# Three plain items instead of two in each up stage, and a scaling row moved to the delta net's output projection

## The chip, the cores and the metric

The kernel runs on one core of a Trainium2 chip. Its engines each work through their own list of instructions in order and meet at semaphores: TensorE (PE, matrix products), VectorE (DVE), ScalarE (ACT), GpSimd (POOL) and SyncE (SP, which here only issues transfers). The metric is the device time of one execution in microseconds.

## The reference

A trunk of two layers over a sequence of 1024 positions with 1024 features, all in float32. Each layer is a mixer and a feed-forward block, both with a residual and a layer norm whose scale, shift and output gain come from a conditioning vector ("ada"):

```python
FFN_HIDDEN = ((8 * D_MODEL // 3 + 255) // 256) * 256   # 2816
FFN_CONV = 3
```

Layer 0 mixes with a gated delta net (projection, causal convolution, chunked recurrence, output projection), layer 1 with a retention. The feed-forward block makes two products of the normalized activations with the up weights, a gate half and an up half of 2816 features each. The gate goes through a causal convolution over three positions and a silu, is multiplied with the up half, and the result goes through the down weights. What the change touches is the up product, and the conditioning's output gain row of layer 0's feed-forward block, a product of the conditioning vector with a 1024 x 1024 part of the ada weights.

## The kernel before

**Arithmetic.** A float32 operand is held as two parts, high and low. `split` (L87 to L90) makes them: ACT copies the high part (L89), DVE subtracts it from the source (L90). `mm3` (L109 to L112) multiplies two such operands with three matmuls of 128 x 128 by 128 x 512.

**Stages** (us in the profiled execution): prologue to 87; delta net to 640; its output projection (`proj_ln`, matmuls at L324) 642 to 771; the first layer's up stage 771 to 1200; its down product (`proj_gen`, L1454) to 1440; retention to 2290; the second layer's up stage 2290 to 2725; its down product to 2952.

**The up stage** is `strassen` (L1173). The activations are cut into blocks of 4 tiles each, called "11", "21", "12", "22" (features by halves of the sequence). The weights come in 22 items, each with two units `ua`, `ub` of 512 KB; `pair_items` lists for each of 11 pairs a gate item and then an up item. An item's four output tiles are made in one of two ways.

- A *plain* item is `side(n, 0)` and `side(n, 1)`. A side multiplies both units (loaded and split whole by `load_w`) with "11" and "21", or with "12" and "22": 2 units x 8 tiles x 3 = 48 matmuls, 96 for both sides.
- `wino` makes an item of 7 block products of 12 matmuls, 84 together, by the scheme of Strassen and Winograd. It needs sums of weight blocks (`psub`, recorded at L1229), a split of each of the seven blocks (`wb`, L89 and L90 again), copies of partial results (L1240) and adds. Four of its products take T1 to T4, sums of activation blocks.

The order at the stage's start: first side of items 1 and 0 (each copied aside by ACT), then `build_T` (L424 to L475), which makes "12" and "22" and returns `rest()`, which makes T1 to T4 tile by tile; second side of item 0; `rest()`; second side of item 1; `wino` for items 2 to 21. T1 and T2 are allocated under the same tag ("hTb", 8 buffers) as "12", so their tiles for k = 2 and 3 are written into buffers of "12" once its last product is over. After a gate item stands its convolution (`conv`, L1573 to L1585: ACT at L1578 and L1584, two L1583 on DVE for each of four tiles), with an up item the product with the gate (L1597) and sums for the down product (L1604). In `wino` the matmuls of a product stand at L110 to L112, or at L1179 where they are added onto an open sum; a gate item's adds are at L1569.

**Work in the background.** `bg_ada` (L219 to L262) queues small units that make the conditioning's rows and columns. A row has two halves of 512 features. For each half eight tiles of 512 KB are loaded by SP (L225) into a tile `mvw` whose tag is `bg_tag[0]`, and DVE adds them up with the vector's entries as scalars (one L235, seven L237); a product with ones sums over the partitions (L259, in plain float32, recorded as two matmuls) and a copy puts the row aside (L260). The queue is worked off one unit at each `bg_step` (L113), two to each `wino` item. `bg_ada(0, 5, "row")` is queued after the output projection and so is done within the first eight of those units; in the first layer four columns of layer 1 (`bg_ada(1, j, "col")`) come behind it.

A scheduler fixes the order of each engine's instructions when the program is built, from the order in which they are written and its estimate of when they are ready; the source order alone doesn't tell it.

Of the kernel before, what the change touches and what calls it, by code (L numbers as in the profile page):

```python
# [24 lines left out]
NF = F // P  # L25
# [8 lines left out]
def trunk_kernel(ctx: ExitStack, tc, A):  # L34
# [82 lines left out]
    bg_tag = ["wr"]  # L117
# [76 lines left out]
    def vcol(name):  # L194
        a, n = VC[name]
        return vc[:, a:a + n]
# [22 lines left out]
    def bg_ada(i, j, kind):  # L219
        box = {}  # L220

        def unit(nh, kp):
            wr = tl(bg_tag[0], [P, 2, HALF], name="mvw")
            c0 = j * D + nh * HALF
            sp.dma_start(wr, A["ada_w"][i, kp * 256:(kp + 1) * 256, c0:c0 + HALF].rearrange("(a p) n -> p a n", p=P))  # L225
            return 2 if bg_tag[0] == "xT" else 1, lambda: work(nh, kp, wr)

        def work(nh, kp, wr):
            if kp == 0:
                box["a"] = tl("ada", [P, HALF])  # L230
            a = box["a"]
            for kk in range(2):
                k = kp * 2 + kk
                if k == 0:
                    dve.tensor_scalar(a, wr[:, 0], e[:, 0:1], None, ALU.mult)  # L235
                else:
                    dve.scalar_tensor_tensor(a, wr[:, kk], e[:, k:k + 1], a, ALU.mult, ALU.add)  # L237
            if kp < KT // 2 - 1:
                return
            if kind == "col":  # L240
                if nh == 0:
                    vecs[i, j] = ct(f"v{i}{j}", [P, KT])
                gs = slice(4 * nh, 4 * nh + 4)
                v, b = vecs[i, j][:, gs], bias_cols(i, j)[:, gs]
                tp, pt = bg_ps[0](), tl("sm2", [P, 4], name="cs")
                for g in range(4):
                    pe.transpose(tp[:, g * P:(g + 1) * P], a[:, g * P:(g + 1) * P], ident)
                for g in range(4):
                    act.activation(a[:, g * P:(g + 1) * P], tp[:, g * P:(g + 1) * P], AF.Copy, accum_out=pt[:, g:g + 1])
                if j in (1, 2, 4):  # L250
                    dve.scalar_tensor_tensor(v, pt, 1.0, b, ALU.add, ALU.add)
                else:
                    dve.tensor_add(v, pt, b)
            else:
                if nh == 0:
                    rows[i, j] = row_load(A["ada_b"][i:i + 1, j * D:(j + 1) * D], ("x", i))
                g = rows[i, j][nh]
                pt = bg_ps[0]()
                pe.matmul(pt, ones, a, start=True, stop=True)  # L259
                dve.scalar_tensor_tensor(g, pt, 1.0, g, ALU.add, ALU.add)  # L260

        for nh in range(2):  # L262
            for kp in range(KT // 2):
                bg.append(lambda nh=nh, kp=kp: unit(nh, kp))
# [290 lines left out]
    xT = {}  # L555
# [614 lines left out]
        dve.tensor_tensor(b, a, b, ALU.add)  # L1170
        return b

    def strassen(hT0, xts, scale, shift, items, tags=("hTb", "hTb", "qkv", "qkv", "aux"), direct=False):  # L1173
        B = {"11": hT0[:4], "21": hT0[4:]}
        nblk = [0]
        nacc = [0]

        def mm_on(*a, **kw):
            return pe.matmul(*a, skip_group_check=True, **kw)  # L1179

        held = {}

        def side(n, s):
            out = []
            for u in items[n][:2]:
                w = held.pop(u.offset, None) or load_w(u)
                if n == 0 and s == 0:
                    held[u.offset] = w
                X = acc_tile()
                for i, b in enumerate((("11", "21"), ("12", "22"))[s]):  # L1190
                    for k in range(4):
                        mm3(X, w, k + 4 * i, B[b][k], i == 0 and k == 0, i == 1 and k == 3)
                out.append(X)
            return out

        ahead, sinks = {}, {}
        for n in (1, 0):
            X = side(n, 0)
            if direct:
                sinks[n] = items[n][2]()  # L1200
                for i in range(2):
                    sinks[n](2 * i, X[i], None)
                continue
            ahead[n] = [tl("cv", [P, 516], name="ah")[:, 0:HALF] for _ in range(2)]
            for t, x in zip(ahead[n], X):
                act.activation(t, x, AF.Copy)
        rest = build_T(B, xts, scale, shift, tags)

        def block(src):
            n = nblk[0]  # L1210
            nblk[0] += 1
            t = tl(("wh", "wl")[n % 2], [P, 2, HALF], F32R, name="wb")
            split(t[:, 0], t[:, 1], src)
            return kn(t[:, 0]), kn(t[:, 1])

        def prod(src, b, onto=None):
            w = block(src)
            if onto is None:
                nacc[0] += 1
                acc = (acc_tile, acc_tile, sc_tile)[nacc[0] % 3]()  # L1220
            else:
                acc = onto
            for k in range(4):
                mm3(acc, w, k, B[b][k], onto is None and k == 0, k == 3, mm_on if onto is not None else pe.matmul)
            return acc

        def psub(x, y, op=ALU.subtract):
            t = mm_tile()
            dve.tensor_tensor(t, x, y, op)  # L1229
            return t  # L1230

        def wino(n, sink):
            ua, ub = items[n][:2]
            wa, wb = tl("wr", [P, D]), tl("wr", [P, D])
            sp.dma_start(wa, ua)
            anchor["wi"] = sp.dma_start(wb, ub)
            a11, a12, a21, a22 = wa[:, hs(0)], wa[:, hs(1)], wb[:, hs(0)], wb[:, hs(1)]
            def copy_of(X, tag="cv"):
                t = tl(tag, [P, 516] if tag == "cv" else [P, HALF], name="pc")[:, 0:HALF]
                act.activation(t, X, AF.Copy)  # L1240
                return t

            X = prod(a11, "11")
            p1 = copy_of(X)
            s1 = psub(a21, a22, ALU.add)
            sink(0, prod(a12, "21"), p1)
            s2 = psub(s1, a11)
            Z = prod(s1, "T1")
            z5 = copy_of(Z)
            s4 = psub(a12, s2)  # L1250
            prod(s2, "T2", X)
            u2 = copy_of(X)
            s3 = psub(a11, a21)
            prod(s4, "22", Z)
            sink(1, Z, u2)
            bg_step()
            prod(s3, "T3", X)
            u3 = copy_of(X, "t2")
            sink(3, X, z5)
            sink(2, prod(a22, "T4"), u3)  # L1260
            bg_step()
            if n > 4:
                row_step()

        bg_tag[0] = "lane"
        for n in range(2):
            if not direct:
                sinks[n] = items[n][2]()
                for i in range(2):
                    sinks[n](2 * i, ahead[n][i], None)  # L1270
            X = side(n, 1)
            for i in range(2):
                sinks[n](2 * i + 1, X[i], None)
            if n == 0:
                rest()
            if items[n][3]:
                items[n][3]()
        for n in range(2, len(items)):
            wino(n, items[n][2]())
            if items[n][3]:  # L1280
                items[n][3]()
        bg_tag[0] = "wr"
        return B
# [249 lines left out]
    def layer_tail(i, mix, wout, xsrc, x_mid, x_out, ln_next, final):  # L1533
        sc2, sh2 = fold(i, 1, 2 * i)
        if i == 0:
            hT0 = []
            get = out_hl(mix)
            G1 = rows[0, 2]
            xts = proj_ln(0, GH, get, wout, xsrc, G1, ("x", i))
            hooks = ln_hooks(0, xts, "hTa", lambda: (sc2, sh2), hT0, x_mid, ("mid", i), BAL["gh"])  # L1540
            xts = proj_ln(1, GH, get, wout, xsrc, G1, ("x", i), hooks=hooks)
            hooks = ln_hooks(1, xts, "hTa", lambda: (sc2, sh2), [], x_mid, ("mid", i))
            for h in hooks[KT:]:
                h()
        else:
            mix.append((sc2, sh2))
            hT0, xts = proj_st(mix[0])
        bg_ada(i, 5, "row")
        bg_gain(2 * i, x_mid, xg[i + 1], "xT")
        if i == 0:  # L1550
            for j in (1, 0, 4, 3):
                bg_ada(1, j, "col")
        cw = vcol(f"ffn_conv{i}")
        cb = vcol(f"ffn_convb{i}")
        ad = dr.tile([NF // 2, 7, P, HALF], F32, tag=f"ad{i}", name=f"ad{i}")
# [51 lines left out]

            return [(up[4 * fp], up[4 * fp + 2], gate_start, conv), (up[4 * fp + 1], up[4 * fp + 3], up_start, None)]

        strassen(hT0, xts, sc2, sh2, [it for fp in range(NF // 2) for it in pair_items(fp)])  # L1610
        while rowq or rowp:
            row_step()
        slots = {"c": "hTa", "x": "qkv"}
# [23 lines left out]
    h0, xts = layer_tail(0, raws, A["gdn_wout"], xin, xs[0], xs[1], next0, False)  # L1637
# [337 lines left out]
```

## Time and profile before

| | |
|---|---|
| runs, us | 2944.8, 2956.14, 2954.41 (median 2954.41) |
| the profiled execution's own time, us | 2954.0 |
| its span in the trace, us | 2952.2 |
| mean granted TensorE clock | 0.982 |
| loads of the ada weights | 80 of 512 KB, 40.96 MB of 344.11 MB read |

The page gives busy times of one execution by engine and the chain of work that ended last, which is followed back from the last instruction to what released it. A timeline row has the start, the duration, the engine, the source line (often that of a helper), the operation with its output and inputs, its count, and in brackets the time that the engine stood idle before it with who ended that. A row of the windows has, for a stretch of time, the busy time of each engine, the granted clock (PEclk, 1.00 is full), and the transfers' share and rate.

### The profile page before, as it was taken

The numbers are of one execution on the slowest core, as the hardware profiler recorded it, in microseconds if no ns is written. First come the engines' busy times: TensorE is split into PE (matmuls) and PEld (weight loads), VectorE is DVE, ScalarE is ACT, GpSimd is POOL, SyncE is SP. The second block draws the span as 40 slices with busy tenths as digits, with TensorE's granted clock in tenths as the row PEclk, the third lists the DMA queues.
The fourth block names the chain that finished last, engine by engine and source line by source line (L and its number), as shares of the span: only waits on it lengthen the run. The fifth ranks groups of instructions, "written<-read, shape, count | busy, mean of one in ns | idle before, by whom it ended". The sixth has DMA issues, their size and how long they took to land.

```text
span 2952.2 us, 38981 instructions
## 1 busy us (share of the span) xinstructions
PE 2822.2 (96%) x13638; PEld 2306.3 (78%) x13638; DVE 2212.5 (75%) x3973; ACT 1316.4 (45%) x2413; POOL 494.4 (17%) x517
## 2 busy tenths in 40 slices
PE   8999898999999999998999999999999899999997
PEld 7787777887787888887878877777777788888886
DVE  5788787656688888958686665666779787777779
ACT  4745565444544444545333332221344544445543
POOL 0312221100013332000000012422202023331001
PEclk9999999999999999999999999999999999999999
DMA  7232222253255655855343364655673353334853
GB/s 277 86 108 68 83 79 80 83 166 138 93 178 173 213 187 191 300 156 176 130 140 121 115 217 154 210 170 164 186 242 125 106 168 128 136 129 161 293 182 114
DMA packets 248276, 459.40 MB, mean 156 GB/s; under 512 B 23632, under 2 KB 77136, under 8 KB 248080
## 3 DMA queue, kind: packets, MB, share of 16 engines
q1 hardware_dynamic: 215680, 405.27, 41.8%
q10 hardware_dynamic: 29760, 43.00, 4.0%
q0 software_dynamic: 2640, 8.65, 0.8%
q8 instruction: 107, 1.75, 0.3%
q14 instruction: 89, 0.73, 0.1%
HBM read 344.11 MB, written 112.72 MB: 155 GB/s over the span
## 4 chain that ended last, share of the span: by engine, by line
PE 73%; DVE 13%; DMA 6%; ACT 4%; issue 2%; POOL 1%; SPq 0%; POOLq 0%; ACTq 0%; DVEq 0%
PE acc L667 15%; PE acc L1179 9%; PE acc L110 5%; PE acc L111 5%; PE acc L112 5%; PE sc L1179 4%; PE sc L667 4%; PE acc L1454 3%; PE mm L667 3%; PE sc L111 2%; PE sc L112 2%; PE sc L110 2%; DVE o L1583 1%; PE mm L1454 1%; PE sc L1454 1%
## 5 line engine op out<-in xcount | busy, mean ns | idle before, releaser
L667 PE MATMUL acc<-hT,wh 128*128 128x512 f32 x960 | 300.2, 394 | 0.0
L1454 PE MATMUL acc<-bb,ab 128*128 128x512 f32 x984 | 236.7, 399 | 12.1 <-DVE bb L90 10.5
L1454 PEld LDWEIGHTS acc<-bb,ab 128*128 128x128 f32 x984 | 186.4, 191 | 56.1 <-DVE bb L90 15.5
L1179 PE MATMUL acc<-T,wb 128*128 128x512 f32 x840 | 203.2, 391 | 6.3 <-DVE wb L90 6.2
L667 PEld LDWEIGHTS acc<-hT,wh 128*128 128x128 f32 x960 | 182.3, 190 | 34.1
L89 ACT ACTIVATE ab<-ar 128x512 fp32r<-128x512 f32 x210 | 130.1, 626 | 166.5 <-PE mm L301 47.8
L667 PE MATMUL acc<-hT,wl 128*128 128x512 f32 x480 | 201.3, 419 | 0.0
L90 DVE TENSOR_TENSOR ab<-ar,ab 128x512 fp32r<-128x512 f32 x210 | 148.5, 713 | 65.2 <-ACT ab L89 65.2
L409 POOL TENSOR_TENSOR xg<-xg,gb 128x512 f32<-128x512 f32 x48 | 62.6, 1304 | 776.3 <-DMA xg<-xs 453.1
L1179 PEld LDWEIGHTS acc<-T,wb 128*128 128x128 f32 x840 | 156.7, 188 | 43.6 <-DVE wb L90 9.0
L90 DVE TENSOR_TENSOR wl<-wr,wh 128x1024 fp32r<-128x1024 f32 x95 | 119.8, 1262 | 88.3 <-ACT wh L89 88.1
L90 DVE TENSOR_TENSOR wb<-wr,wb 128x512 fp32r<-128x512 f32 x162 | 115.8, 720 | 71.5 <-ACT wb L89 71.4
L89 ACT ACTIVATE wh<-wr 128x1024 fp32r<-128x1024 f32 x95 | 100.7, 1061 | 146.4 <-PE acc L667 66.9
L90 DVE TENSOR_TENSOR wb<-mm,wb 128x512 fp32r<-128x512 f32 x216 | 145.8, 684 | 26.5 <-ACT wb L89 25.7
L1604 POOL TENSOR_TENSOR o<-o 128x512 f32<-128x512 f32 x80 | 111.7, 1405 | 287.6 <-ACT pc L1240 190.0
L1583 DVE SCALAR_TENSOR_TENSOR o<-g,vc,o 128x512 f32<-128x512 f32 (+2 forms) x176 | 154.7, 896 | 5.3 <-ACT o L1578 4.7
L89 ACT ACTIVATE wb<-mm 128x512 fp32r<-128x512 f32 x216 | 124.1, 595 | 59.8 <-DVE mm L1229 55.0
L1240 ACT ACTIVATE pc<-acc 128x512 f32<-128x512 f32 x143 | 84.8, 593 | 145.3 <-PE acc L1179 93.1
L89 ACT ACTIVATE wb<-wr 128x512 fp32r<-128x512 f32 x162 | 98.4, 627 | 104.5 <-DMA wr<-in_ffn_up 49.3
L667 PE MATMUL acc<-wh,hT 128*128 128x512 f32 x384 | 139.2, 425 | 2.9 <-DVE vv L90 1.7
L110 PE MATMUL acc<-T,wb 128*128 128x512 f32 x292 | 116.0, 397 | 9.4 <-DVE wb L90 9.4
L488 DVE SCALAR_TENSOR_TENSOR qkv<-raw,vc,qkv 128x512 f32<-128x512 f32 x144 | 111.7, 780 | 11.5 <-ACT qkv L486 10.7
(639 smaller groups left out, 7488.1 us busy)
## 6 DMA issues: line engine op xcount, KB each, us to landing
wr<-in_ffn_up SPq DMA_DIRECT2D x92, 512.0 KB, 4.3
mvw<-in_ada_w SPq DMA_DIRECT2D x80, 512.0 KB, 4.5
ad<-o SPq DMA_DIRECT2D x154, 256.0 KB, 3.1
ar<-ad SPq DMA_DIRECT2D x154, 256.0 KB, 3.8
Br<-in_ffn_down SPq DMA_DIRECT2D x88, 256.0 KB, 3.4
wr<-in_ret_wv SPq DMA_DIRECT2D x32, 512.0 KB, 4.1
ar<-od SPq DMA_DIRECT2D x56, 256.0 KB, 5.3
xs<-xt ACTq DMA_DIRECT2D x24, 512.0 KB, 3.8
```

Source lines behind the costliest of these rows:

```text
L89: act.activation(dst_h, src, AF.Copy)
L90: eng.tensor_tensor(dst_l, src, dst_h, ALU.subtract)
L110: mm(acc, wl[:, k], hl[0], start=first, stop=False)
L111: mm(acc, wh[:, k], hl[1], start=False, stop=False)
L112: mm(acc, wh[:, k], hl[0], start=False, stop=last)
L488: dve.scalar_tensor_tensor(oh, raw[:, 3 - j:515 - j], w[:, 3 - j:4 - j], oh, ALU.mult, ALU.add)
L667: pq(pe.matmul(out, lhsT, rhs, start=start, stop=stop), cost)
L1179: return pe.matmul(*a, skip_group_check=True, **kw)
L1240: act.activation(t, X, AF.Copy)
L1454: return pe.matmul(*args, skip_group_check=True, **kw)
L1583: dve.scalar_tensor_tensor(tv, gv[:, c0 - j:c1 - j], w[:, 2 - j:3 - j], tv, ALU.mult, ALU.add)
L1604: (dve if fp == 0 else pool).tensor_tensor(o[d], o[x], o[y], op)
```

## The change

```diff
-    def strassen(hT0, xts, scale, shift, items, tags=(...), direct=False):
+    def strassen(hT0, xts, scale, shift, items, tags=(...), direct=False, plain=2):
...
                 w = held.pop(u.offset, None) or load_w(u)
-                if n == 0 and s == 0:
+                if n in (0, 2) and s == 0:
                     held[u.offset] = w
...
-        for n in range(2, len(items)):
+        for n in range(2, plain):
+            sink = items[n][2]()
+            for s in range(2):
+                for i, x in enumerate(side(n, s)):
+                    sink(2 * i + s, x, None)
+            if items[n][3]:
+                items[n][3]()
+        for n in range(plain, len(items)):
             wino(n, items[n][2]())
...
         if i == 0:
+            bg_ada(0, 5, "row")
+            bg_tag[0] = "xT"
             hT0 = []
             get = out_hl(mix)
...
             for h in hooks[KT:]:
                 h()
+            bg_tag[0] = "wr"
         else:
             mix.append((sc2, sh2))
             hT0, xts = proj_st(mix[0])
-        bg_ada(i, 5, "row")
         bg_gain(2 * i, x_mid, xg[i + 1], "xT")
         if i == 0:
             for j in (1, 0, 4, 3):
                 bg_ada(1, j, "col")
+        else:
+            bg_ada(1, 5, "row")
...
-        strassen(hT0, xts, sc2, sh2, [it for fp in range(NF // 2) for it in pair_items(fp)])
+        strassen(hT0, xts, sc2, sh2, [it for fp in range(NF // 2) for it in pair_items(fp)], plain=3)
```

In both layers' up stages item 2, the gate item of the second pair, is made by plain products with all four blocks; its weights are kept from its first side to its second (`held`). `wino` begins with item 3. A plain item makes no background steps, so that 38 of them remain in an up stage where there were 40. A third call of `strassen`, in the retention, keeps two plain items.

In layer 0 the row `bg_ada(0, 5, "row")` is queued ahead of the output projection, with its tiles under the tag "xT" (two buffers), and the steps of the projection work it off; the up stage keeps the four columns of layer 1. In layer 1 the row stays in the up stage, queued behind the gain.

More of the change, by code (lines that the diff above doesn't have):

```diff
@@ L1171, in c_of, with strassen @@
         return b
-    def strassen(hT0, xts, scale, shift, items, tags=("hTb", "hTb", "qkv", "qkv", "aux"), direct=False):
+    def strassen(hT0, xts, scale, shift, items, tags=("hTb", "hTb", "qkv", "qkv", "aux"), direct=False, plain=2):
         B = {"11": hT0[:4], "21": hT0[4:]}
```

## The prediction

> **What bounds the kernel now.** I read the page first: part 1 for the engines, part 4 for the chain that ended last.
>
> ```profile
> PE 2822.2 (96%) x13638; PEld 2306.3 (78%) x13638; DVE 2212.5 (75%) x3973; ACT 1316.4 (45%) x2413; POOL 494.4 (17%) x517
> PE 73%; DVE 13%; DMA 6%; ACT 4%; issue 2%; POOL 1%; SPq 0%; POOLq 0%; ACTq 0%; DVEq 0%
> ```
>
> TensorE (PE) is busy 96% of 2952.2 us and is 73% of the chain. So work taken off VectorE (DVE) is worth something only where PE waits for it. Next I asked for busy time in stretches around the places that the change touches: the delta net's output projection, the start of the first up stage, its wait, its steady part, and the last two again in the second layer.
>
> ```profile
> core 0: us, PE busy (x) PEld busy (x) DVE busy (x) ACT busy (x) POOL busy (x), PEclk, DMA share, GB/s
> 640.00:771.00 131.00, 122.88 (x563) 100.36 (x562) 85.93 (x152) 57.51 (x79) 9.92 (x10) 0.97 0.48 159
> 787.20:811.90 24.70, 19.20 (x83) 15.13 (x81) 21.79 (x33) 14.46 (x24) 0.00 (x0) 0.96 0.20 65
> 811.90:842.00 30.10, 29.24 (x118) 23.71 (x119) 28.56 (x47) 16.03 (x28) 0.00 (x0) 0.92 0.50 167
> 842.00:1190.00 348.00, 346.83 (x1531) 283.64 (x1530) 303.94 (x459) 163.61 (x323) 103.48 (x84) 1.00 0.57 189
> 2343.10:2374.00 30.90, 30.41 (x122) 24.47 (x123) 29.20 (x47) 16.32 (x29) 0.00 (x0) 0.90 0.52 169
> 2374.00:2725.00 351.00, 350.92 (x1542) 288.90 (x1541) 267.61 (x393) 158.66 (x273) 104.66 (x84) 1.00 0.41 142
> ```
>
> In the steady parts PE works 346.83 of 348.00 us and 350.92 of 351.00: DVE at 87% there (303.94 of 348.00) costs nothing. Only the starts have anything to win. The matmul timeline at the first start shows it:
>
> ```profile
> 795.18 0.39 PE L110 MATMUL acc<-12_7183,wl 128*128 128x512 f32 x1
> ...
> 806.85 0.39 PE L112 MATMUL sc<-hT,wb 128*128 128x512 f32 x1
> 811.93 0.79 PE L110 MATMUL acc<-T,wb 128*128 128x512 f32 x1 [4.69 <-DVE wb L90]
> 812.52 0.63 PE L111 MATMUL acc<-T,wb 128*128 128x512 f32 x1
> 812.95 0.63 PE L112 MATMUL acc<-T,wb 128*128 128x512 f32 x1
> ...
> 816.67 0.40 PE L112 MATMUL acc<-T,wb 128*128 128x512 f32 x1
> 817.90 3.02 PE L1179 MATMUL acc<-T,wb 128*128 128x512 f32 x12 [0.84 <-DVE wb L90]
> ...
> 825.97 2.88 PE L1179 MATMUL acc<-T,wb 128*128 128x512 f32 x12
> 828.69 0.39 PE L112 MATMUL acc<-T,wb 128*128 128x512 f32 x1
> ```
>
> Columns are start, duration, operation, idle time before it and who ended it. From 795.18 PE runs the last unit of item 1's second side, then item 2's products by a11 and a12, and at 807.24 (806.85 + 0.39) it waits 4.69 us for the split of item 2's third block, the one for T1. The 12 matmuls after the wait start 0.43 apart (812.95 - 812.52) and are over at 817.07, after 5.14 us; the same twelve later take 2.88. So a wait costs its 4.69, then 2.26 of slow matmuls (granted clock 0.92 in the 811.90 row), then 0.84 for the next block. The second layer repeats it:
>
> ```profile
> 2343.11 0.80 PE L110 MATMUL acc<-T,wb 128*128 128x512 f32 x1 [4.69 <-DVE wb L90]
> ...
> 2347.97 0.63 PE L112 MATMUL acc<-T,wb 128*128 128x512 f32 x1
> 2349.08 2.99 PE L1179 MATMUL acc<-T,wb 128*128 128x512 f32 x12 [0.49 <-DVE wb L90]
> ```
>
> That is 4.69, then 5.49 - 2.88 = 2.61 (2347.97 + 0.63 - 2343.11 = 5.49), then 0.49. All that the change can win at the two starts is 4.69 + 2.26 + 0.84 + 4.69 + 2.61 + 0.49 = 15.58 us.
>
> What makes the block late is the DVE timeline of the same stretch:
>
> ```profile
> 796.74 1.39 DVE L90 TENSOR_TENSOR T<-bt,T 128x512 fp32r<-128x512 f32 x2 [0.32 <-ACT T L89]
> ...
> 805.69 0.69 DVE L90 TENSOR_TENSOR T<-bt,T 128x512 fp32r<-128x512 f32 x1 [0.32 <-ACT T L89]
> 806.30 0.75 DVE L1583 SCALAR_TENSOR_TENSOR o<-g,vc,o 128x511 f32<-128x511 f32 x1
> 807.27 0.69 DVE L1569 TENSOR_TENSOR g<-sc,pc 128x512 f32<-128x512 f32 x1 [0.22 <-PE sc L112]
> 807.88 3.39 DVE L1583 SCALAR_TENSOR_TENSOR o<-g,vc,o 128x512 f32<-128x512 f32 x5
> 811.19 0.68 DVE L90 TENSOR_TENSOR wb<-mm,wb 128x512 fp32r<-128x512 f32 x1
> ```
>
> T1 and T2 for k = 2, 3 are written into buffers of the "12" blocks (one tag), so their splits start only when the last plain product by "12" lets them go; the L89 copy ahead of the split at 796.74 is released by a matmul. Behind these stand the other T blocks, the gate sum, six convolution steps (L1583) and only then the block that PE needs.
>
> **The change part by part.** *Plain item 2.* Seven products of 12 matmuls become two units of two sides, 96 matmuls: +12 per layer, +24. Twelve take 828.69 - 825.97 = 2.72 us, 0.227 each; all lie on PE's path: **+5.4 us**.
>
> Its weights are split as two tiles per layer, in place of seven blocks:
>
> ```profile
> L90 DVE TENSOR_TENSOR wl<-wr,wh 128x1024 fp32r<-128x1024 f32 x95 | 119.8, 1262 | 88.3 <-ACT wh L89 88.1
> L90 DVE TENSOR_TENSOR wb<-mm,wb 128x512 fp32r<-128x512 f32 x216 | 145.8, 684 | 26.5 <-ACT wb L89 25.7
> L89 ACT ACTIVATE wh<-wr 128x1024 fp32r<-128x1024 f32 x95 | 100.7, 1061 | 146.4 <-PE acc L667 66.9
> ```
>
> Each copy waits for PE to finish with the tile before it (idle "<-PE"), and split is 1.06 + 1.26 = 2.32 us; PE has 24 matmuls, 5.5 us, of the other unit meanwhile. I take 0; with no cover it would be 2 x 2.32 per layer. DVE is spared 15 short operations (seven splits, four sums, four adds) per layer and gets two longer splits, which by the reading of the steady rows wins nothing there.
>
> *The wait.* The last plain product by "12" is now that of item 2's second side. In the order in which the built program's instructions stand, T1 and T2 for k = 2, 3 again wait for it, and DVE's line-up behind them is the same: T splits and sums, then the gate/up sum of the next item (item 3), then L1583 six times, then item 3's split for T1. PE's cover from the release is again 24 matmuls of a unit and 24 by a11 and a12. So the wait moves one item later and stays. One thing differs: of the six L1583 one stood ahead of the sum in what was free time, now all six stand behind it: 3.39 / 5 = 0.68 more. I put the wait at 5.4 us, +0.7 per layer: **+1.4**. Bounds: as short as 1.3 if the scheduler's six convolution steps (4.07) find room earlier after all; as long as 8.1 (4.69 + 3.39) if five more such steps get in.
>
> The second wait shrinks, since one step of the second scaling row no longer stands between the two blocks in layer 0, and the split can run in the longer first wait: 0.84 and 0.49 to about 0.2: **-0.9** (bounds -1.3 and 0). The slow twelve stay: both gaps of 4.69 were followed by them, while those of 0.84 and 0.49 were not: **0** (bound -4.9).
>
> The Trainium skill, "TensorE: Matmul & The Clock Gate", section "Part 1: The HAM clock gate", says that the clock drops to half after at least one idle window of about 3.4 us and that this window runs freely. By that a gap of 5.4 us may, or may not, hold a whole window; if neither did, the sum would be 4.9 us lower, 2956. Two gaps out of two here paid, so I keep the cost.
>
> *The row.* Its work for layer 0 is 8 loads of 512 KB for each half, two L235 and fourteen L237, and two ones-matmuls (L259, recorded as two each) with their copies (L260).
>
> ```profile
> L237 DVE SCALAR_TENSOR_TENSOR ada<-mvw,e,ada x140: 732/746/1616, 72.1 to 2414.6; 128x512 f32<-128x512 f32 x140
> L235 DVE TENSOR_SCALAR ada<-mvw,e x20: 476/480/489, 71.1 to 2391.7; 128x512 f32<-128x512 f32 x20
>   DMA mvw<-in_ada_w: 10.7, 7
> mvw<-in_ada_w SPq DMA_DIRECT2D x80, 512.0 KB, 4.5
> 858.84 1.02 PE L259 MATMUL mm<-ada,ones 128*128 128x512 f32 x2
> ```
>
> In the up stage it took 2 x 0.48 + 14 x 0.75 = 11.4 us of DVE under a full PE; PE's part, about 1.0 us for each half, is paid wherever it stands: **0**. The loads go to SP from the prologue on, in two buffers, and the scheduler sets the first half's sums in the delta net's tail and the second half's between the weight splits of the output projection. Each half is 0.48 + 7 x 0.75 = 5.7 us:
>
> ```profile
> 579.80 0.42 DVE L908 TENSOR_SCALAR T<-mm 32x256 f32<-32x256 f32 x1 [6.84 <-PE mm L667]
> 684.29 1.23 DVE L90 TENSOR_TENSOR wl<-wr,wh 128x1024 fp32r<-128x1024 f32 x1 [2.33 <-ACT wh L89]
> 688.62 0.69 DVE L90 TENSOR_TENSOR hl<-raw,hl 128x512 fp32r<-128x512 f32 x1 [2.50 <-ACT hl L89]
> ```
>
> The first half fits into the 6.84 us that DVE idles before 579.80. The second meets 2.33 + 2.50 = 4.8 us of idle time at 684 to 690; 0.9 is over, and DVE is free 45 us of that stage's 131 (85.93 busy). I take **+1** of 0 to 3. Cover gone, PE would wait 5.7 us.
>
> Sum, against the profiled execution's own 2954.0: 5.4 + 1.4 - 0.9 + 1 = +6.9, **2961 us**. The median of the runs shown, 2954.41, stands at the same place. By its bounds this case lies between 2952 (both waits 4.1 shorter) and 2968 (both 2.7 longer, the row 2 more).
>
> **The rivals.** *B, the wait is gone (the other side: not slower).* If item 2's 96 matmuls let DVE, spared of its block splits, finish T and convolution before item 3's third block, all 15.6 us go: 2954.0 - 15.6 + 5.4 + 1 = 2945. For it: DVE has less to do in that item. Against: the release is the same last use of "12", and it decides only if DVE's T chain is shorter than the 48 matmuls behind it; at 795 to 811 it was 4.7 longer.
>
> *C, the row's loads hold the projection.* Each next load waits until DVE frees one of two buffers, lands 4.5 us later, and DVE stands in order ahead of the weight and activation splits that PE needs; SP's weight loads for the projection stand behind it. The seven waits for such loads so far took 10.7 in all, 1.5 each. Six loads of the second half at 1.5 give 9, of which the 1 is counted: 2961 + 8 = 2969. For it: only two buffers. Against: loads go out early. It decides from where DVE's lag passes the idle 4.8.
>
> *D, item 2 starves.* If the plain item's weight splits are not covered, 2.3 us per layer for the second unit: 2961 + 4.6 = 2966. For it: each copy waits for PE's last use. *E, the row isn't where the change says*: by the build order half of it is in the delta net's tail, which changes no term.
>
> **How the numbers follow.** Forecast 0.66, B 0.14, C 0.12, D 0.08. The range must leave out no more than 0.2: it takes the forecast's bounds, D, all of C's lower part and B's own time: 2944 to 2970. The forecast's own range is 2952 to 2968. A measurement of this kernel can tell about 0.5% from no change, 14.8 us, so faster is below 2939.6 and slower above 2969.2. B at 2945 reaches the first only with luck (a third of it: 0.05); C passes the second in over half, D and the forecast seldom (0.07 + 0.01 + 0.04 = 0.12); the rest, 0.83, is no change.
>
> **What will show it.** In the changed kernel: no wait over 1 us inside item 2's matmuls (else D); a row with about 5.4 idle, released by DVE's split, at the first product by T of item 3, some 22 us later than now (96 x 0.227 = 21.8), with twelve matmuls 0.43 apart behind it, in both layers. If this row is missing or under 2 us, B holds and my reading of the release was wrong. L237 near 565 to 580 and 674 to 690; waits there "<-DMA mvw" over 3 us, and a 640 to 771 stretch longer than 132, show C. The steady stretches should be unchanged to 1 us. A change over 10 us anywhere else makes the whole forecast wrong.

## The result, and the profile after

| | before | after |
|---|---|---|
| median of the runs, us | 2951.67 (5 runs) | 2992.83 (5 runs) |
| lowest and highest, us | 2942.52, 2956.14 | 2987.21, 2994.34 |
| profiled execution, its span, us | 2954.0, 2952.2 | 2994.34, 2992.6 |

The ratio is 1.0145, 95% interval 1.013 to 1.016: 41 us slower, where 2961 had been forecast. (The median of before is over five runs, two more than those shown ahead.) Line numbers of the changed kernel are larger by 7 to 11 behind `strassen`: L1569, L1583, L1596, L1597, L1604 of before are L1580, L1594, L1607, L1608, L1615 after.

The page's engines and the chain that ended last, after:

```profile
PE 2834.0 (95%) x13662; PEld 2303.3 (77%) x13662; DVE 2213.5 (74%) x3947; ACT 1311.4 (44%) x2403; POOL 500.7 (17%) x517
PE 25%; DVE 7%; DMA 2%; issue 1%; POOL 1%; ACT 1%; SPq 0%; DVEq 0%; POOLq 0%; ACTq 0%
```

PE has 24 matmuls more and 12 us more busy time, against 40 us of span. This chain covers only some 37% of the span; it could not be followed further back, so it says nothing of where the time went. Stretches do. I take an up stage from the first matmul of `build_T` (L455) to the first of the down product (L299), from the timelines of both:

| stretch | before, us | after, us | difference |
|---|---|---|---|
| up to the first up stage | 778.2 | 776.9 | -1.3 |
| first up stage | 421.6 | 450.0 | +28.4 |
| down product, to the retention's `build_T` | 255.2 | 257.5 | +2.3 |
| retention, to the second up stage | 853.7 | 853.2 | -0.5 |
| second up stage | 415.9 | 425.8 | +9.9 |
| from there to the end | 227.6 | 229.2 | +1.6 |

So the moved row cost nothing, and 38.3 of 40.4 us lie in the two up stages. Their starts first: PE's timeline after, at item 3's product by T1 in the first layer and then the second.

```profile
833.29 0.80 PE L110 MATMUL acc<-T,wb 128*128 128x512 f32 x1 [5.51 <-DVE wb L90]
...
836.02 0.52 PE L110 MATMUL acc<-T,wb 128*128 128x512 f32 x1
836.38 0.40 PE L111 MATMUL acc<-T,wb 128*128 128x512 f32 x1
...
837.30 0.39 PE L112 MATMUL acc<-T,wb 128*128 128x512 f32 x1
838.61 3.01 PE L1179 MATMUL acc<-T,wb 128*128 128x512 f32 x12 [0.91 <-DVE wb L90]
```

```profile
2394.66 0.80 PE L110 MATMUL acc<-T,wb 128*128 128x512 f32 x1 [5.50 <-DVE wb L90]
...
2399.52 0.43 PE L112 MATMUL acc<-T,wb 128*128 128x512 f32 x1
2399.98 2.33 PE L1179 MATMUL acc<-T,wb 128*128 128x512 f32 x9
```

The wait moved one item later and grew from 4.69 to 5.5, where 5.4 had been forecast, and slow matmuls follow it. But that is 0.8 us for each layer, and the stages lost 28.4 and 9.9. The windows of the steady parts, after:

```profile
860.00:1220.00 360.00, 341.86 (x1478) 271.65 (x1479) 297.94 (x438) 160.61 (x327) 109.99 (x84) 1.00 0.50 170
2500.00:2740.00 240.00, 240.00 (x1060) 198.81 (x1059) 183.22 (x263) 111.85 (x191) 80.32 (x64) 1.00 0.39 138
```

In the first layer PE now idles 18 of 360 us, with DVE at 83% (297.94 of 360), less than the 87% of before: neither engine is busy all the time. In the second layer, from 2500 on, PE is busy throughout; the background row's last sum there starts at 2484.8. One up item on PE, first layer, shows the idle time:

```profile
1108.00 0.50 PE L110 MATMUL acc<-T,wb 128*128 128x512 f32 x1 [0.83 <-DVE wb L90]
1111.21 3.02 PE L1179 MATMUL sc<-T,wb 128*128 128x512 f32 x12 [0.20 <-DVE wb L90]
1115.22 0.96 PE L1179 MATMUL acc<-22_7230,wb 128*128 128x512 f32 x3 [0.99 <-ACT pc L1240]
```

Waits of 0.1 to 1.7 us, most of them for single block splits and the others for ACT's copies of partial results, go on from 857 to 1177 us, to the end of the background columns. Why DVE is late without being full is seen in its own timeline. First an up item of before: the sum s1 = a21 + a22 at 1082.01 needs the item's second load, and the split of a22 at 1094.52 is the last use of that buffer, after which the next item's load can go out.

```profile
1058.05 0.16 DVE L253 TENSOR_TENSOR v<-cs,vc 128x4 f32<-128x4 f32 x1 [1.77 <-ACT ada L249]
1058.13 0.48 DVE L235 TENSOR_SCALAR ada<-mvw,e 128x512 f32<-128x512 f32 x1
...
1061.17 0.70 DVE L1229 TENSOR_TENSOR mm<-wr 128x512 f32<-128x512 f32 x1 [1.07 <-DMA wr<-in_ffn_up]
...
1082.01 0.70 DVE L1229 TENSOR_TENSOR mm<-wr 128x512 f32<-128x512 f32 x1
1082.62 0.68 DVE L1597 TENSOR_TENSOR o<-o,acc 128x512 f32<-128x512 f32 x1
1083.21 0.69 DVE L1229 TENSOR_TENSOR mm<-mm,wr 128x512 f32<-128x512 f32 x1
...
1094.52 0.68 DVE L90 TENSOR_TENSOR wb<-wr,wb 128x512 fp32r<-128x512 f32 x1
```

The gate item ahead of it starts at 1061.17 with a wait for its load; a finished column's last step (L253) and the next one's first (L235) stand ahead of that wait, where DVE has nothing else to do. The up item has no background between s1 and the split of a22: 1094.52 + 0.68 - 1082.01 = 13.2 us. After:

```profile
1095.50 0.69 DVE L90 TENSOR_TENSOR wb<-wr,wb 128x512 fp32r<-128x512 f32 x1 [1.95 <-ACT wb L89]
1098.71 0.70 DVE L1229 TENSOR_TENSOR mm<-wr 128x512 f32<-128x512 f32 x1 [2.52 <-DMA wr<-in_ffn_up]
1099.32 0.16 DVE L251 SCALAR_TENSOR_TENSOR v<-cs,vc 128x4 f32<-128x4 f32 x1
1099.40 1.59 DVE L235 TENSOR_SCALAR ada<-mvw,e 128x512 f32<-128x512 f32 x1
1100.91 0.69 DVE L1229 TENSOR_TENSOR mm<-mm,wr 128x512 f32<-128x512 f32 x1
1101.51 0.65 DVE L272 TENSOR_TENSOR fs<-v,vc 128x8 f32<-128x8 f32 x1
...
1102.76 0.74 DVE L237 SCALAR_TENSOR_TENSOR ada<-mvw,e,ada 128x512 f32<-128x512 f32 x1
...
1104.62 1.53 DVE L237 SCALAR_TENSOR_TENSOR ada<-mvw,e,ada 128x512 f32<-128x512 f32 x2
...
1111.67 1.61 DVE L1229 TENSOR_TENSOR mm<-wr 128x512 f32<-128x512 f32 x1
...
1116.70 0.68 DVE L90 TENSOR_TENSOR wb<-wr,wb 128x512 fp32r<-128x512 f32 x1
```

This is an up item (L1607, L1608 stand in it). Now the column's last step and most of the next sums fall between its s1 and its a22: 1116.70 + 0.68 - 1098.71 = 18.7 us. DVE idles 1.95 us behind ACT's copy of a block, which itself waited 1.62 us for the item's first load, then 2.52 us for the second load, and after that does the background work while PE waits for blocks. The load into the buffer that the split of a22 lets go is issued at 1117.42, and the sum that needs it, the next s1, starts 4.4 us later, at 1121.86. So the item takes 1121.86 - 1098.71 = 23.2 us of a chain through DVE and the weight buffers, where PE needs 84 x 0.227 = 19.1. Counted from one issue of the second weight load (L1236) to the next, between 859 and 1161 us, the up items take 22.2 to 24.1 us and the gate items 17.7 to 20.2; before it was 18.1 to 19.3 and 19.9 to 22.2. After, a gate item doesn't make up what the up item ahead of it lost.

The columns' work comes in a rhythm: of the eight sums (L235, L237) of half a column, six fall to one item, along with the small steps that finish a half, and two to the next, counted between issues of the second weight load. Before, the six fell to gate items, after to up items. The columns began at item 6 before, behind the row's four items; after they begin at item 3. That became theory A.

### The profile page after: what moved, and what is told of

It reads as the page before. It is cut to its first block, busy times and chain, and to the rows that moved or that the text cites. A ratio compares the mean times of both kernels' runs of the same rounds, so it can differ in the third digit from the quotient of the medians.

```text
span 2992.6 us, 38968 instructions
## 1 busy us (share of the span) xinstructions
PE 2834.0 (95%) x13662; PEld 2303.3 (77%) x13662; DVE 2213.5 (74%) x3947; ACT 1311.4 (44%) x2403; POOL 500.7 (17%) x517
## 3 DMA queue, kind: packets, MB, share of 16 engines
q1 hardware_dynamic: 215680, 405.27, 40.4%
## 5 line engine op out<-in xcount | busy, mean ns | idle before, releaser
L90 DVE TENSOR_TENSOR wl<-wr,wh 128x1024 fp32r<-128x1024 f32 x99 | 127.0, 1284 | 92.9 <-ACT wh L89 92.6
L409 POOL TENSOR_TENSOR xg<-xg,gb 128x512 f32<-128x512 f32 x48 | 66.2, 1379 | 762.8 <-DMA xg<-xs 454.7
L1615 POOL TENSOR_TENSOR o<-o 128x512 f32<-128x512 f32 x80 | 116.8, 1469 | 330.1 <-DVE o L1608 244.5
L1594 DVE SCALAR_TENSOR_TENSOR o<-g,vc,o 128x512 f32<-128x512 f32 (+2 forms) x176 | 157.0, 911 | 6.7 <-ACT o L1589 5.9
L90 DVE TENSOR_TENSOR wb<-mm,wb 128x512 fp32r<-128x512 f32 x208 | 139.5, 684 | 23.7 <-ACT wb L89 22.8
L110 PE MATMUL acc<-T,wb 128*128 128x512 f32 x284 | 114.4, 403 | 19.9 <-DVE wb L90 16.6
L237 DVE SCALAR_TENSOR_TENSOR ada<-mvw,e,ada 128x512 f32<-128x512 f32 x140 | 114.2, 815 | 11.2 <-DMA mvw<-in_ada_w 10.5
```

Of the source, the lines that this page charges most:

```text
L90: eng.tensor_tensor(dst_l, src, dst_h, ALU.subtract)
L110: mm(acc, wl[:, k], hl[0], start=first, stop=False)
L409: pool.tensor_tensor(x, x, gb[0], ALU.mult)
L1594: dve.scalar_tensor_tensor(tv, gv[:, c0 - j:c1 - j], w[:, 2 - j:3 - j], tv, ALU.mult, ALU.add)
L1615: (dve if fp == 0 else pool).tensor_tensor(o[d], o[x], o[y], op)
```

## The experiments

Four theories were put against each other. A: the kind of item on which the background work falls. B: item 3's longer wait puts DVE behind, and it doesn't catch up. C: the moved row. D: the rotation of accumulators and block buffers, which two counters in `strassen` set and which begins at item 3 instead of 2.

**1. Three plain items alone, and 2. the row alone.** The first puts `bg_ada(i, 5, "row")` back into both up stages, the second leaves out `plain=3`.

> Three plain items, the row back in the up stage. Theory A (what matters is which kind of item the background columns of the first up stage fall on: they began at a gate item, 6, and begin at an up item in the changed kernel; here the row takes items 3 to 6 and the columns begin at item 7, an up item): still slow, 2980 to 3000. Theory B (the longer wait at item 3 puts DVE behind and it never catches up): 2980 to 3000 too. Theory C (the moved row's loads and sums are the cause): about 2961. Theory D (the rotation of accumulators and weight-block buffers, shifted by one item): 2980 to 3000.

> Two plain items, the row moved. The columns begin at item 2, a gate item. A, B and D: like before, 2945 to 2957, and no row of waits along the first up stage. C: 2975 to 2995.

Measured: 3000.85 (ratio 1.017, 1.0151 to 1.0189) and 2949.8 (0.9991, 0.9978 to 1.0003). C falls: the row's move alone changes nothing that can be told, and the loss comes with the third plain item. With three plain items the row in the up stage costs 8 us more (3000.85 against 2992.83; the first up stage is 456.4 us long instead of 450.0), where with two its move was worth nothing.

**3. The background steps.** Two steps in the plain item, so that the columns begin at a gate item.

```diff
             for s in range(2):
                 for i, x in enumerate(side(n, s)):
                     sink(2 * i + s, x, None)
+                bg_step()
```

> The changed kernel with two background steps in the plain item, so that the first layer's columns begin at item 2, a gate item, as they began at one before. A: the small waits along the first up stage go, 2955 to 2968; the 5.5 us wait at item 3's third block stays. B, C and D: 2985 to 2998.

Measured: 2984.79 (1.0111, 1.0095 to 1.0126), a miss for A's number, and 0.2 us from the range of the other three theories. But the rows are those that A expected: nearly all the small waits are gone, the 5.5 us wait stays, and the first up stage is 431.3 us long instead of 450.0. In their place a second long wait stands at item 4, 4.78 us in the first layer and 5.01 in the second, behind item 3's 5.5: the early steps give DVE more work just where it is already behind.

**4. The rotation.**

```diff
-        nblk = [0]
-        nacc = [0]
+        nblk = [7 * (plain - 2)]
+        nacc = [4 * (plain - 2)]
```

> The changed kernel with the two counters that choose accumulators and weight-block buffers started where they would stand after one item by seven products, so that every later item uses the same kinds as before. D: 2955 to 2970. A, B and C: 2985 to 2998.

Measured: 2987.07 (1.0119, 1.0104 to 1.0134); the first up stage stays at 452.2 us with its waits. D is not the cause.

**5. Two plain items, but the columns at an up item.** The second experiment's kernel, where item 2 makes no steps (in the retention's stage its second step is left out as well).

```diff
-            bg_step()
+            if n > 2 or direct:
+                bg_step()
...
-            bg_step()
+            if n > 2:
+                bg_step()
```

> Two plain items and the row moved, as in the second experiment, but item 2 by seven products makes no background steps in the two up stages, so that the columns begin at item 3, an up item, as in the changed kernel, while the start of the stage is that of before. A (the kind of item on which the background falls): the small waits come back along the first up stage, 2962 to 2972. B (they follow from the longer wait at item 3): 2944 to 2956, like the second experiment.

Measured: 2975.86 (1.0089, 1.0061 to 1.0118), 4 us above A's range, but 20 above B's and 26 above the second experiment, without any plain item 2 and with the long wait in its old place and size (item 2, 4.69 us). The first up stage grew from 421.6 to 442.9. This decides between A and B. The windows of the second and of this kernel, one stretch each:

```profile
860.00:1200.00 340.00, 338.24 (x1491) 276.08 (x1490) 285.81 (x433) 160.69 (x325) 97.88 (x80) 1.00 0.53 176
```

```profile
860.00:1200.00 340.00, 322.86 (x1397) 256.39 (x1397) 284.07 (x414) 150.76 (x310) 102.71 (x81) 1.00 0.52 175
```

PE's idle time goes from 1.8 to 17.1 us at the same DVE load. DVE's timeline of the fifth kernel has the picture of the changed one: a wait for the load, and the background behind s1.

```profile
1014.73 0.70 DVE L1229 TENSOR_TENSOR mm<-wr 128x512 f32<-128x512 f32 x1 [1.75 <-DMA wr<-in_ffn_up]
1015.33 0.16 DVE L253 TENSOR_TENSOR v<-cs,vc 128x4 f32<-128x4 f32 x1
1015.41 0.48 DVE L235 TENSOR_SCALAR ada<-mvw,e 128x512 f32<-128x512 f32 x1
1015.80 0.69 DVE L1229 TENSOR_TENSOR mm<-mm,wr 128x512 f32<-128x512 f32 x1
...
1034.12 0.68 DVE L90 TENSOR_TENSOR wb<-wr,wb 128x512 fp32r<-128x512 f32 x1
```

**6. Steps and rotation together**, the edits of 3 and 4.

> Changed kernel with the two background steps in the plain item and the two counters set back, both edits of the first round together. If the rotation makes the new waits of 1.0 and 1.8 us at the start of each down product and the steps the small waits: 2973 to 2982, with up stages like the third experiment's (431 and 427 us) and no wait over 1 us at the start of the down products. If the rotation edit's 6 us of the first round came from elsewhere in the up stage: 2985, like the third experiment.

Measured: 2978.65 (1.0089, 1.0054 to 1.0125), in the first range, though not by its rows alone: the wait at item 4 grew to 7.59 and 7.46 us and the up stages to 435.8 and 429.5, while the part from the first up stage's end to the retention fell from 258.7 (third experiment) to 253.3.

**7. The plain item's sides exchanged**, so that "12" is let go 48 matmuls sooner.

```diff
-                if n in (0, 2) and s == 0:
+                if (n, s) in ((0, 0), (2, 1)):
...
-            for s in range(2):
+            for s in (1, 0):
```

> Changed kernel, but the plain item 2 makes its second side (blocks 12 and 22) before its first (11 and 21), so that 48 more matmuls, 10.9 us, stand between the last plain use of the 12 blocks and item 3's third block. The wait of 5.5 us goes in both layers, with the slow twelve matmuls behind it: at least 2 x 7.8 = 16 us less than the changed kernel. A: the small waits of the first up stage stay, 2968 to 2980. B: they go as well, 2950 to 2962.

Measured: 2975.07 (1.0088, 1.0059 to 1.0117). The second up stage, with little background, is 415.1 us long instead of 425.8. In the first the wait at item 3 is gone too, but small waits run on as before and it is 440.0. They don't come from that wait: B falls a second time.

**8. Exchange, steps and rotation.**

> The sixth and the seventh experiment's edits together. A: both the long waits and the small ones go, 2938 to 2955, which would be no slower than before. B: as the seventh experiment, within 5 us.

Measured: 2955.35 (1.0011, 0.9996 to 1.0026), 0.35 us above A's range. The early steps still make a wait at item 4, 4.89 and 3.18 us. So the columns had to be put on gate items without more background at the start.

**9. Exchange, rotation, and no steps in item 3; 10. the last alone; 11. exchange and no steps.** No step in item 3 lets the columns begin at item 4, a gate item.

```diff
-            bg_step()
+            if n > plain or direct:
+                bg_step()
```

(at both places in `wino`)

> Changed kernel with the second side of item 2 first, the two counters set back, and no background steps in item 3, so that the first layer's columns begin at item 4, a gate item, without more background work at the start of the stage. A (background on the up items makes the small waits, item 3's long wait is a separate cost): no wait over 2 us after item 2, up stages of about 418 and 413 us, 2940 to 2952. If the wait at item 4 of the third, sixth and eighth experiments comes from item 2 by plain products itself and not from the early steps: a wait of 3 to 5 us stays there, 2950 to 2960.

> Changed kernel with no background steps in item 3 and nothing else. A: the small waits of the first up stage go, the 5.5 us waits at item 3 stay, up stages of about 430 and 424 us, 2966 to 2976. If the early steps of the third experiment were what helped there: 2988 to 2996.

> The ninth experiment without the counters set back. If the rotation makes the waits at the start of the down products: 3 to 7 us above the ninth, with those waits (0.3 to 1.8 us) in both layers. If not: within 2 us of it.

Measured: 2944.17 (0.9973, 0.996 to 0.9986), 2972.65 (1.007, 1.0055 to 1.0084) and 2948.9 (0.9993, 0.9982 to 1.0003). The ninth and tenth are within what A expected, the eleventh within what the rotation's waits at the down products would give. The tenth differs from the changed kernel in the background's place alone, and its first up stage is 429.2 us long, 20.8 less. Its DVE timeline has a gate item with the column's end ahead of the wait for the load again, as before, and PE's window is near full:

```profile
1062.75 0.16 DVE L251 SCALAR_TENSOR_TENSOR v<-cs,vc 128x4 f32<-128x4 f32 x1 [1.77 <-ACT ada L249]
1062.83 0.48 DVE L235 TENSOR_SCALAR ada<-mvw,e 128x512 f32<-128x512 f32 x1
...
1065.43 0.70 DVE L1229 TENSOR_TENSOR mm<-wr 128x512 f32<-128x512 f32 x1 [0.80 <-DMA wr<-in_ffn_up]
```

```profile
860.00:1200.00 340.00, 335.06 (x1481) 273.70 (x1480) 292.48 (x441) 160.80 (x325) 101.73 (x83) 1.00 0.56 183
```

In the ninth, PE goes from item 3's block for "21" to the one for T1 without a gap, and its up stages are 415.3 and 413.2 us long (before: 421.6, 415.9):

```profile
827.09 0.39 PE L112 MATMUL acc<-hT,wb 128*128 128x512 f32 x1
827.32 0.39 PE L110 MATMUL acc<-T,wb 128*128 128x512 f32 x1
```

It is the only version that is faster than both kernels beyond its interval, by 0.3% of the kernel before. On the rotation: the eleventh, like the changed kernel, waits at the start of the down product, and the ninth does not. The changed kernel's two rows, then the eleventh's:

```profile
1229.40 0.70 PE L299 MATMUL acc<-bb,ab 128*128 128x512 f32 x2 [0.99 <-DVE ab L90]
1232.92 0.50 PE L299 MATMUL acc<-bb,ab 128*128 128x512 f32 x1 [1.81 <-DVE ab L90]
```

```profile
1199.26 0.50 PE L299 MATMUL acc<-bb,ab 128*128 128x512 f32 x1 [1.81 <-DVE ab L90]
```

The medians of the two differ by 4.7 us and their intervals overlap by a little. Two more pairs differ in the rotation alone: from the changed kernel to the fourth experiment it is worth 5.8 us (2992.83 - 2987.07), from the third to the sixth 6.1 (2984.79 - 2978.65). All three point the same way; the size is only roughly known. Why the choice of accumulators makes the down product's first splits late was not tried.

## Why the prediction was wrong

The step that failed is the first one: "DVE at 87% there (303.94 of 348.00) costs nothing. Only the starts have anything to win." From that came that the steady stretches would be unchanged to 1 us, and that a background step less or more in the up stage has no price. The cover of which that step spoke was real for the order of before, and the change replaced the order. It took eight units of background out of the first layer's up stage and two steps away, and I counted the units without asking on which items the other 32 would come to lie. As I read the rows, PE's wait for DVE here hangs on the chain from one weight load to the next, and what stands inside that chain counts, at 83% load as at 87%. With the place put right and nothing else (tenth experiment) 20.2 us of the 41 are gone (2992.83 - 2972.65), and the place put wrong in a kernel with two plain items costs 26. That the place of the background decides is shown; that it does so by the path through the weight buffers is not, since no run changed their number (two) or moved a load.

Point by point:

- *Plain item, 24 matmuls, +5.4.* The 24 are there (13662 against 13638). No wait inside item 2 (D doesn't hold).
- *The wait, +1.4.* Mechanism and size were right: 5.51 and 5.50 against 4.69, item 3, released by DVE's split, behind six L1583. The moved wait was forecast at 5.4.
- *The second wait, -0.9.* It came to 0.91 and none, against 0.84 and 0.49: -0.4.
- *The slow twelve, 0.* In the first layer only some seven were slow: 837.30 + 0.39 - 833.29 = 4.40 us, 1.5 over the normal 2.88 instead of 2.26. In the second, 2399.98 - 2394.66 = 5.32, start to start, against 2.72: 2.6, as before. In the fifth experiment a gap of 4.69 us was followed by two matmuls at the normal pace and then by slow ones (start at 816.07, 1.7 us lost); in the eighth a gap of 3.18 us, at 2388.42, by none that was slow. The Trainium skill, "TensorE: Matmul & The Clock Gate", section "Part 1: The HAM clock gate", calls the clock's window free-running; that two gaps of 5.5 us are followed by slow stretches of different length agrees with it.
- *What the sum lacked at the starts.* With the small waits gone, the up stages of the tenth experiment are still 7.6 and 8.3 us longer than before, where the terms above give about 3 for each. Most of the rest lies in waits at items 4 and 5 (1.62, 0.46 and 1.93 us in the first layer, 0.78 and 2.16 in the second), which I had not priced. That DVE leaves the long wait behind with more to do is my reading. That the long wait and this lag go together is borne out by the exchange of sides: it saves 23.75 us (tenth to eleventh, 2972.65 - 2948.9), more than the tenth's two waits with their slow matmuls, 5.50 + 5.50 + 1.87 + 1.47 = 14.34.
- *The row, +1.* The stage starts 1.3 us earlier after, and the second experiment shows no change: 0. The sums stand in the delta net's tail and in the projection as told; rival C doesn't hold, nor does B, and E changes nothing. C was also priced too high: a half of a row or column has four loads, not eight (80 loads stand against 20 L235, one for each half), so with two buffers two waits of 1.5 us were at stake and not six.
- *The down products.* I had no term for their starts; they cost 2.3 and 1.6 us.

So about half of the loss is the background's place, most of the other half the longer start with the lag behind it, and the rest the down products. None of the rivals had the first.

## What to carry to other kernels

A busy share below 100% doesn't make an engine's work free: ask where its fill-in work stands against its waits for loads, and whether a change shifts the rhythm by one item. Before costing a moved or dropped step at nothing, compare the order on that engine item by item in the steady part, not only at the place of the edit. And where a change lengthens a phase to hide a wait, look at which of its halves holds the resource: exchanging the two sides of the plain item took it from 20 us of loss (tenth experiment) to none (eleventh).

## What was not expected of the hardware

A two-operand sum on DVE that mostly takes 0.70 us took 1.61 at 1111.67, and L235, 0.48 at 1058.13 before, took 1.59 at 1099.40. Such rows are no less common before: an L1583 of 0.74 took 1.77 at 1052.64. The traces show what goes along with it. Between 850 and 1180 us, of the DVE operations that have a row of their own, 24 take longer than 1.05 us after and 23 before, and each of them overlaps a sum on GpSimd (L409, L410, L1604, or L1615 after); of the 230 and 243 that overlap none, not one is so long. Overlap alone isn't enough, since 59 and 74 others overlap such a sum and keep their time, and no run took GpSimd's sums away.
